# Attention weights transposed in pairs of tiles, eight transposes in a row, and multiplied with the values in pairs

## The chip, the cores and the metric

The kernel runs on one core of one Trainium2 chip. The metric is the device time of one execution in microseconds; the time of a kernel is the median over its runs. The engines are TensorE (PE in the profile, with PEld for its weight loads), VectorE (DVE), ScalarE (ACT), GpSimd (POOL) and SyncE (SP, which here only issues transfers).

## The reference

One layer with two kinds of heads over 2048 tokens of width 1024. The normalised input is projected once. Group A is stick-breaking attention with 16 heads of width 64, group B a chunked state-space scan; both are gated, normalised, and mapped back by one output projection. The change is in group A:

```python
z = jnp.einsum('bqhd,bkhd->bhqk', qi, kf) * scale
mask = key_pos[None, :] < q_pos[:, None]
log_keep = jnp.where(mask, jax.nn.log_sigmoid(-z), 0.0)
rest = lax.cumsum(log_keep, axis=3, reverse=True) - log_keep
w = jnp.where(mask, jnp.exp(jax.nn.log_sigmoid(z) + rest), 0.0)
return jnp.einsum('bhqk,bkhd->bqhd', w, vf)
```

A query reads the keys before it from the nearest to the farthest, and each key takes a sigmoid share of what the nearer ones left. The kernel computes this with a scan over the keys that runs backwards: the scanned value `w` is what has been given to all keys up to one place, and the values are taken as differences of neighbouring rows, so that `w` itself can be multiplied with them.

## The kernel before

The program has three stages: the state-space group of the first 1024 tokens with its projections, then `attention` (L450), then the state-space group of the other half and the output projection. Only `attention` is concerned.

**Segments.** Attention goes through 32 segments `(H, p, q)` (L452): the half `H` of the tokens, the pair of heads `p`, and the block `q` of 512 queries in that half. For each of the two heads of a pair it goes over the key tiles of 512 keys, from the block's own (the diagonal one) back to the first, `Q + 1` of them with `Q = 2 * H + q`. A key tile has four steps, one for each 128 queries. That makes 8, 16, 24 or 32 steps in a segment and 640 in all.

**A step**, `z_step` (L594), computes one tile of 128 queries by 512 keys: two products into a bank `z` of PSUM (L601, L602; on the diagonal a third one adds the mask, L604), two sigmoids on ACT (L606 into `be`, L607 in place in `z`), and the scan on DVE (L610), which reads both and writes `w`. `z` has two banks, so a score waits until the scan of two steps before is over. On the diagonal the tiles are narrower: 128, 256, 384 and 512 keys.

**Transposes**, `t_step` (L615). Before `w` meets the values, its keys must lie on the partitions. For each 128 keys `j` of a key tile, PE transposes the 128 columns of the four `w` of that tile, four transposes into one bank `t` (L619; fewer on the diagonal). ACT casts the bank to `th` in fp32r (L622), DVE subtracts to get the rest `tl` (L624), and then the bank is free. There are two banks `t`, and the projection stage uses the same two for its own transposes of queries and keys (L524, with L530 and L531 to empty them).

**Products with the values**, `av_step` (L632): `V` with `th` (L636) and with `tl` (L637), added up in the bank `av` over all key tiles of a head. There is one such bank. At the end of a head ACT copies one half of it into `y` (L642), DVE adds the other (L643), and only then may the next head's first product write.

**The order.** Each step puts its `j` into the queue `tq`. `advance` (L654), called once a step, takes the oldest entry for a transposition as soon as six wait (`LAG`), and then multiplies the oldest transposed tile as soon as more than two of them wait (`AVLAG`). So a step issues one score, one group of four transposes, and two products. Between the steps `fill` brings in work of the next segments, by a balance of estimated times (L701 to L705): the projection of queries, keys and values (L473 to L475, bank `pj`), the gate (L245 to L247), the transposes of `stage_b`. The last segments have little or none of it. The instructions then pass a scheduler, which orders each engine's instructions ahead of time; on the chip each engine keeps that order.

The numbers of banks and the two lags stand here:

```python
PSB = {"z": 2, "t": 2, "av": 1, "pj": 3}
LAG = 6
AVLAG = 2
```

Of the kernel before, what the change touches and what calls it, by code (L numbers as in the profile page):

```python
# [30 lines left out]
LAG = 6  # L31
# [4 lines left out]
UNIT = 0.55  # L36
CS = (0, 2, 4)
FF = (1.05, 1.35)
AVLAG = 2


def f32(t):
    return t.bitcast(F32)
# [3 lines left out]
def hybrid_layer_kernel(ctx: ExitStack, tc: tile.TileContext, x, norm_w, wA, wP0, wP, wZ, wdt, vec, w_out, out):  # L47
# [16 lines left out]
    def ps(tag):  # L64
        return psum.tile([P, 512], F32, name=tag, bufs=PSB[tag])
# [171 lines left out]
    def projector(hx):  # L237
        hh, hl = [h[0] for h in hx], [h[1] for h in hx]

        def proj_steps(pj, wts, cs, q, m=P):  # L240

            wh, wl = wts
            for kt in range(KT):
                a, b = wh[kt][:, cs], wl[kt][:, cs]
                te.matmul(pj[:m], a, hh[q][:, kt, :], start=(kt == 0), stop=False)  # L245
                te.matmul(pj[:m], a, hl[q][:, kt, :], start=False, stop=False)  # L246
                te.matmul(pj[:m], b, hh[q][:, kt, :], start=False, stop=(kt == KT - 1))  # L247
                yield

        def proj_t(wts, cs, q, m=P):  # L250
            pj = ps("pj")
            drain(proj_steps(pj, wts, cs, q, m))
            return pj
        return proj_t, proj_steps
# [195 lines left out]
    def attention(ap_, wp, hp, hx):  # L450
# [164 lines left out]
        def t_step(h, c, j, ws):  # L615
            lo = j if c == h.Q else 0
            tp = ps("t")
            for i in range(lo, 4):
                te.transpose(tp[:, i * P:(i + 1) * P], ws[i][:, j * P:(j + 1) * P], ident)  # L619
            rs = slice(lo * P, 512)  # L620
            th = ap_.tile([P, 512], F32R, name="th", bufs=4)
            sc.copy(th[:, rs], tp[:, rs])  # L622
            tl = ap_.tile([P, 512], F32R, name="tl", bufs=3)
            ve.tensor_tensor(tl[:, rs], tp[:, rs], f32(th[:, rs]), op=ALU.subtract)  # L624
            if lo == 3:

                gp.memset(f32(th[:, 256:384]), 0.0)
                gp.memset(f32(tl[:, 256:384]), 0.0)
                rs = slice(256, 512)
            return th, tl, rs  # L630

        def av_step(h, c, j, V, tt):  # L632
            th, tl, rs = tt
            if c == h.Q and j == 0:
                h.av = ps("av")
            te.matmul(h.av[:, rs], V[:, j, :], th[:, rs], start=(c == h.Q and j == 0), stop=False)  # L636
            te.matmul(h.av[:, rs], V[:, j, :], tl[:, rs], start=False, stop=(c == 0 and j == 3))  # L637
            if c == 0 and j == 3:
                own = slice(h.e * 64, h.e * 64 + 64)
                oth = slice(64 - h.e * 64, 128 - h.e * 64)  # L640
                y = h.y
                sc.copy(y[own], h.av[oth])  # L642
                ve.tensor_tensor(y[own], h.av[own], y[own], op=ALU.add)  # L643
                gp.tensor_mul(y[own], y[own], h.gz[own])  # L644
                if h.e == 1:
                    nc.sync.dma_start(ysb_d[h.p, :, h.Q * 512:(h.Q + 1) * 512], y)
# [5 lines left out]
        tq, aq = [], []  # L652

        def advance():  # L654
            if len(tq) >= LAG:
                h, c, j, ws, V = tq.pop(0)
                aq.append((h, c, j, V, t_step(h, c, j, ws)))
            if len(aq) > AVLAG:
                av_step(*aq.pop(0))

        for n, (H, p, q) in enumerate(segs):
            fill = fill_for(n)
# [24 lines left out]
            for e in range(2):  # L687
                h = Head()
                h.p, h.e, h.Q, h.y, h.gz = p, e, Q, y, gzs[H, p, q]
                h.AB = made[H, p, q][0][e]  # L690
                prev = [None] * 4
                for c in range(Q, -1, -1):
                    if todo:
                        fetch(*todo.pop(0))
                    M, V = mv.pop((e, c))
                    ws = []
                    for i in range(4):
                        z_step(h, c, i, M, ws, prev)
                        tq.append((h, c, i, ws, V))
                        advance()  # L700
                        due += scale * tau[step % len(tau)] - core[step % len(tau)]  # L701
                        step += 1
                        while due >= UNIT:
                            next(fill, None)
                            due -= UNIT  # L705
            drain(fill)
        while tq or aq:
            if aq:
                av_step(*aq.pop(0))
            if tq:  # L710
                h, c, j, ws, V = tq.pop(0)
# [73 lines left out]
    with tc.tile_pool(name="sp1", bufs=1, side="right") as sp:  # L785
        chunks, gates, _ = ssd(1, sp, wp, *projector(hx))
# [67 lines left out]
```

## Time and profile before

| | |
|---|---|
| Median of 3 runs | 2744.19 us (2741.96 to 2746.96) |
| The profiled execution | 2747.84 us, its span 2745.6 us |
| PE busy | 2592.6 us, 94% of the span |
| PE's weight loads busy | 2138.9 us, 78% |
| DVE busy | 2016.6 us, 73% |
| ACT busy | 1647.5 us, 60% |
| POOL busy | 845.8 us, 31% |
| Scans (L610, 128x512, with a carried value) | 384 of 1278 ns, 490.7 us |
| Transposes of attention weights (L619) | 2176, 346.6 us |
| Casts to `th` (L622) | 640, 339.0 us |
| Subtractions to `tl` (L624) | 640, 376.9 us |

A matmul's start is recorded and its end is modelled; several are in the pipe at once. So the distance from one start to the next tells what a matmul costs, and its duration does not: the 2176 transposes have a mean duration of 275 ns, yet follow each other at 0.11 us. An idle time in brackets at the end of a row names what ended it.

### The profile page before, as it was taken

The numbers are of one execution on the slowest core, as the hardware profiler recorded it, in microseconds if no ns is written. First come the engines' busy times: TensorE is split into PE (matmuls) and PEld (weight loads), VectorE is DVE, ScalarE is ACT, GpSimd is POOL, SyncE is SP. The second block draws the span as 40 slices with busy tenths as digits, with TensorE's granted clock in tenths as the row PEclk, the third lists the DMA queues.
The fourth block names the chain that finished last, engine by engine and source line by source line (L and its number), as shares of the span: only waits on it lengthen the run. The fifth ranks groups of instructions, "written<-read, shape, count | busy, mean of one in ns | idle before, by whom it ended". The sixth has DMA issues, their size and how long they took to land.

```text
span 2745.6 us, 40149 instructions
## 1 busy us (share of the span) xinstructions
PE 2592.6 (94%) x13858; PEld 2138.9 (78%) x13858; DVE 2016.6 (73%) x3160; ACT 1647.5 (60%) x3551; POOL 845.8 (31%) x844
## 2 busy tenths in 40 slices
PE   7998999999999999999999999999999896989999
PEld 5876788888888778787878787877776774778877
DVE  6566337767776777968696868688997667877766
ACT  4557446666666666868686867677886456331221
POOL 1456232322333222121212121212112456351553
PEclk9999999999999999999999999999999998999999
DMA  3225642222322422122212121222121136574553
GB/s 114 62 74 144 228 122 65 78 76 83 93 81 86 116 73 70 58 81 58 81 55 85 53 86 51 84 56 74 57 70 39 49 94 184 184 219 146 153 166 115
DMA packets 207627, 265.16 MB, mean 97 GB/s; under 512 B 18384, under 2 KB 127200, under 8 KB 207424
## 3 DMA queue, kind: packets, MB, share of 16 engines
q1 hardware_dynamic: 188992, 229.04, 28.1%
q10 hardware_dynamic: 18432, 33.56, 4.2%
q8 instruction: 109, 1.79, 0.3%
q14 instruction: 94, 0.77, 0.1%
HBM read 178.00 MB, written 59.38 MB: 86 GB/s over the span
## 4 chain that ended last, share of the span: by engine, by line
PE 53%; DVE 25%; issue 7%; ACT 7%; DMA 4%; POOL 3%; SPq 0%; ACTq 0%; DVEq 0%; POOLq 0%
DVE w L610 8%; PE t L619 5%; PE pj L475 4%; PE pj L474 4%; PE pj L473 4%; DVE tl L624 4%; PE pj L247 3%; PE pj L246 3%; PE pj L245 3%; PE av L636 3%; PE z L601 3%; PE av L637 2%; PE z L602 2%; PE pj L762 2%; PE pj L760 2%
## 5 line engine op out<-in xcount | busy, mean ns | idle before, releaser
L610 DVE TENSOR_TENSOR_SCAN w<-z,w,be 128x512 f32<-128x512 f32 x384 | 490.7, 1278 | 135.1 <-ACT z L607 132.5
L606 ACT ACTIVATE be<-z 128x512 f32<-128x512 f32 (+3 forms) x640 | 343.7, 537 | 328.9 <-PE z L604 166.0
L624 DVE TENSOR_TENSOR tl<-t,th 128x512 fp32r<-128x512 f32 (+3 forms) x640 | 376.9, 589 | 9.5 <-ACT th L622 7.6
L622 ACT CAST th<-t 128x512 fp32r<-128x512 f32 (+3 forms) x640 | 339.0, 530 | 31.8 <-PE t L619 29.5
L619 PE MATMUL t<-ident,w 128*128 128x128 f32 x2176 | 346.6, 275 | 9.8 <-DVE tl L624 3.8
L473 PE MATMUL pj<-wh,hh 128*128 128x384 f32 (+1 forms) x1024 | 349.9, 342 | 0.0
L475 PE MATMUL pj<-wh,hl 128*128 128x384 f32 (+1 forms) x1024 | 346.8, 339 | 0.0
L474 PE MATMUL pj<-wl,hh 128*128 128x384 f32 (+1 forms) x1024 | 346.7, 339 | 0.0
L607 ACT ACTIVATE z<-z 128x512 f32<-128x512 f32 (+3 forms) x640 | 341.1, 533 | 0.2
L610 DVE TENSOR_TENSOR_SCAN w<-z,be 128x128 f32<-128x128 f32 (+3 forms) x256 | 209.8, 819 | 170.3 <-ACT z L607 141.3
L619 PEld LDWEIGHTS t<-ident,w 128*128 128x128 f32 x2176 | 255.1, 141 | 71.7 <-DVE tl L624 16.7
L133 POOL TENSOR_TENSOR wl<-wraw,wh 128x384 fp32r<-128x384 f32 (+3 forms) x163 | 169.4, 1050 | 440.8 <-ACT wh L132 238.7
L644 POOL TENSOR_TENSOR y<-y,gz 64x512 f32<-64x512 f32 x64 | 82.9, 1296 | 531.1 <-DVE y L643 530.6
L473 PEld LDWEIGHTS pj<-wh,hh 128*128 128x128 f32 x1024 | 192.9, 188 | 12.5 <-ACT hh L173 0.2
L474 PEld LDWEIGHTS pj<-wl,hh 128*128 128x128 f32 x1024 | 193.0, 189 | 12.0
L475 PEld LDWEIGHTS pj<-wh,hl 128*128 128x128 f32 x1024 | 193.0, 188 | 0.7
L246 PE MATMUL pj<-hl,zh 128*128 128x512 f32 x432 | 175.3, 406 | 0.0
L245 PE MATMUL pj<-hh,zh 128*128 128x512 f32 x432 | 173.3, 401 | 0.0
L247 PE MATMUL pj<-hh,zl 128*128 128x512 f32 x432 | 172.2, 399 | 0.0
L636 PE MATMUL av<-th,V 128*128 128x512 f32 (+2 forms) x384 | 155.3, 405 | 12.1 <-DVE y L643 11.2
L601 PE MATMUL z<-M,AB 128*128 128x512 f32 (+2 forms) x384 | 141.4, 368 | 10.7 <-DVE w L610 8.5
L637 PE MATMUL av<-tl,V 128*128 128x512 f32 (+2 forms) x384 | 141.1, 368 | 0.0
(244 smaller groups left out, 6060.5 us busy)
## 6 DMA issues: line engine op xcount, KB each, us to landing
wraw<-in_wP_dram SPq DMA_DIRECT2D x112, 192.0 KB, 2.5
wk<-acs_scr SPq DMA_DIRECT2D x64, 256.0 KB, 3.4
AB<-AB SPq DMA_DIRECT2D x128, 128.0 KB, 2.4
Mc<-kc_scr ACTq DMA_DIRECT2D x64, 256.0 KB, 2.7
Vc<-vc_scr ACTq DMA_DIRECT2D x64, 256.0 KB, 2.6
wraw<-in_wZ_dram SPq DMA_DIRECT2D x54, 256.0 KB, 2.6
wraw<-in_wA_dram SPq DMA_DIRECT2D x44, 192.0 KB, 2.3
ea<-acs_scr SPq DMA_DIRECT2D x32, 256.0 KB, 4.4
```

The lines of the kernel that those rows point to most:

```text
L245: te.matmul(pj[:m], a, hh[q][:, kt, :], start=(kt == 0), stop=False)
L246: te.matmul(pj[:m], a, hl[q][:, kt, :], start=False, stop=False)
L247: te.matmul(pj[:m], b, hh[q][:, kt, :], start=False, stop=(kt == KT - 1))
L473: te.matmul(pj[:, :n], a, wh[kt][:, 0:n], start=(kt == 0), stop=False)
L474: te.matmul(pj[:, :n], a, wl[kt][:, 0:n], start=False, stop=False)
L475: te.matmul(pj[:, :n], b, wh[kt][:, 0:n], start=False, stop=(kt == KT - 1))
L606: sc.activation(be[:, :nk], zp[:, :nk], AF.Sigmoid, scale=0.125)
L607: sc.activation(zp[:, :nk], zp[:, :nk], AF.Sigmoid, scale=-0.125)
L610: ve.tensor_tensor_scan(w[:, 0:nk][:, ::-1], zp[:, 0:nk][:, ::-1], be[:, 0:nk][:, ::-1], 0.0 if diag else prev[i][:, 0:1], ALU.mult, ALU.add)
L619: te.transpose(tp[:, i * P:(i + 1) * P], ws[i][:, j * P:(j + 1) * P], ident)
L622: sc.copy(th[:, rs], tp[:, rs])
L624: ve.tensor_tensor(tl[:, rs], tp[:, rs], f32(th[:, rs]), op=ALU.subtract)
```

## The change

`advance` waits until `tq` holds at least six entries and an even number. Then it first multiplies all tiles that are transposed (two of them), and then transposes two more. `AVLAG` goes. The queue so drains two steps' worth at every second step.

```diff
--- before.py
+++ after.py
@@ -36,7 +36,6 @@
 UNIT = 0.55
 CS = (0, 2, 4)
 FF = (1.05, 1.35)
-AVLAG = 2
 
 
 def f32(t):
@@ -652,11 +651,13 @@
         tq, aq = [], []
 
         def advance():
-            if len(tq) >= LAG:
-                h, c, j, ws, V = tq.pop(0)
-                aq.append((h, c, j, V, t_step(h, c, j, ws)))
-            if len(aq) > AVLAG:
-                av_step(*aq.pop(0))
+
+            if len(tq) >= LAG and len(tq) % 2 == 0:
+                while aq:
+                    av_step(*aq.pop(0))
+                for _ in range(2):
+                    h, c, j, ws, V = tq.pop(0)
+                    aq.append((h, c, j, V, t_step(h, c, j, ws)))
 
         for n, (H, p, q) in enumerate(segs):
             fill = fill_for(n)
```

From the deleted line up to `advance`, lines have a number less by one in the changed kernel: scores L600 and L601, scan L609, transposes L618, cast L621, subtraction L623, products L635 and L636.

Uninterrupted groups of attention transposes in the order of PE: 639 before (447 of four, one of seven, the others smaller, on the diagonal) and 451 after (103 of eight, 91 of seven, 32 of five or six, 48 of four, 177 smaller).

PE, a step of the last segment, where no other work is left. `Mc` and `V` are keys and values, `AB` the queries. Before:

```order
L601 MATMUL z<-Mc,AB 128x512
L602 MATMUL z<-Mc,AB 128x512
L619 MATMUL t<-ident,w 128x128 x4
L637 MATMUL av<-tl,V 128x512
L636 MATMUL av<-th,V 128x512
L601 MATMUL z<-Mc,AB 128x512
```

After, two steps:

```order
L600 MATMUL z<-Mc,AB 128x512
L601 MATMUL z<-Mc,AB 128x512
L635 MATMUL av<-th,V 128x512
L600 MATMUL z<-Mc,AB 128x512
L601 MATMUL z<-Mc,AB 128x512
L636 MATMUL av<-tl,V 128x512
L635 MATMUL av<-th,V 128x512
L618 MATMUL t<-ident,w 128x128 x2
L636 MATMUL av<-tl,V 128x512
L618 MATMUL t<-ident,w 128x128 x6
```

Each score was followed by a group of four and two products. Now two scores stand with one product between them, and all eight transposes behind the second score, with the rest of the products ahead of and among them.

DVE at the same place, with buffer numbers (the scan is shown as SCALAR_TENSOR_TENSOR). Before:

```order
L610 SCALAR_TENSOR_TENSOR w_23303<-z_23297,w_23222,be_23300 128x512
L624 TENSOR_TENSOR tl_23312<-t_23305,th_23310 128x512
L610 SCALAR_TENSOR_TENSOR w_23322<-z_23316,w_23244,be_23319 128x512
L624 TENSOR_TENSOR tl_23331<-t_23324,th_23329 128x512
L610 SCALAR_TENSOR_TENSOR w_23341<-z_23335,w_23266,be_23338 128x512
L624 TENSOR_TENSOR tl_23350<-t_23343,th_23348 128x512
```

After:

```order
L609 SCALAR_TENSOR_TENSOR w_23314<-z_23308,w_23236,be_23311 128x512
L609 SCALAR_TENSOR_TENSOR w_23322<-z_23316,w_23244,be_23319 128x512
L623 TENSOR_TENSOR tl_23335<-t_23328,th_23333 128x512
L623 TENSOR_TENSOR tl_23344<-t_23337,th_23342 128x512
L609 SCALAR_TENSOR_TENSOR w_23352<-z_23346,w_23276,be_23349 128x512
L609 SCALAR_TENSOR_TENSOR w_23360<-z_23354,w_23284,be_23357 128x512
```

Scan and subtraction took turns; now two scans are followed by two subtractions.

DVE at the end of a head, in a segment of two key tiles (650 to 694 us in the profile). The next head's first product stands on PE, in both kernels, behind the score that the scan of 128x512 reads; `y` is what it waits for. Before:

```order
L610 SCALAR_TENSOR_TENSOR w_6680<-z_6673,be_6677 128x384
L624 TENSOR_TENSOR tl_6688<-t_6682,th_6686 128x384
L643 TENSOR_TENSOR y_6199<-av_6573,y_6199 64x512
L610 SCALAR_TENSOR_TENSOR w_6711<-z_6704,be_6708 128x512
L624 TENSOR_TENSOR tl_6718<-t_6713,th_6716 128x256
```

After (`qkt` and `qky` are small steps of a normalisation, `raw` its last one):

```order
L609 SCALAR_TENSOR_TENSOR w_6651<-z_6644,be_6648 128x256
L105 SCALAR_TENSOR_TENSOR qkt_6611<-qkx_6609,qky_6610 128x16
L642 TENSOR_TENSOR y_6209<-av_6566,y_6209 64x512
L106 TENSOR_TENSOR qkt_6611<-qkt_6611,qky_6610 128x16
L623 TENSOR_TENSOR tl_6667<-t_6660,th_6665 128x512
L107 SCALAR_TENSOR_TENSOR qky_6610<-qkt_6611,qky_6610 128x16
L623 TENSOR_TENSOR tl_6675<-t_6669,th_6673 128x384
L501 TENSOR_TENSOR raw_6327<-raw_6327,qky_6610 128x1024
L609 SCALAR_TENSOR_TENSOR w_6693<-z_6686,be_6690 128x384
L609 SCALAR_TENSOR_TENSOR w_6711<-z_6704,be_6708 128x512
```

The addition to `y` stood between the scans of 128x384 and 128x512; now it stands one scan earlier, ahead of that of 128x384.

## Rows read from the trace of the kernel before

**Rows 1.** Windows, attention: us, busy time by engine, clock, DMA share, GB/s.
```profile
386.00:2101.00 1715.00, 1650.06 (x9276) 1392.81 (x9275) 1347.88 (x2033) 1215.48 (x2696) 390.11 (x455) 0.99 0.26 74
```

**Rows 2.** Windows: a segment of two key tiles, one of four.
```profile
650.00:694.00 44.00, 42.41 (x249) 37.10 (x248) 33.28 (x56) 30.73 (x73) 9.37 (x12) 1.00 0.18 50
...
1515.90:1584.30 68.40, 65.95 (x367) 53.52 (x367) 61.64 (x88) 56.00 (x121) 12.86 (x16) 1.00 0.19 55
```

**Rows 3.** Waits in attention, PE's weight loads: total us, times, longest.
```profile
PEld z L601 <- DVE w L610: 90.3, 170, 2.4
...
PEld av L636 <- DVE y L643: 23.3, 44, 0.9
PEld t L619 <- DVE tl L624: 16.7, 46, 1.4
...
PEld t L524 <- DVE tl L624: 3.9, 14, 0.8
```

**Rows 4.** Waits in attention: idle time of PE's products.
```profile
PE z L601 <- DVE w L610: 28.0, 76, 2.0
PE av L636 <- DVE y L643: 11.2, 24, 0.7
```

**Rows 5.** Timeline of PE (start, us, instruction): a group of four.
```profile
453.88 0.60 PE L619 MATMUL t<-ident,w 128*128 128x128 f32 x4
454.23 0.48 PE L636 MATMUL av<-th,V 128*128 128x512 f32 x1
454.55 0.39 PE L637 MATMUL av<-tl,V 128*128 128x512 f32 x1
454.78 0.33 PE L473 MATMUL pj<-wh,hh 128*128 128x384 f32 x1
```

**Rows 6.** Timeline of PE: a run of eight.
```profile
479.93 1.04 PE L524 MATMUL t<-ident,raw 128*128 128x128 f32 x8
480.73 0.36 PE L601 MATMUL z<-M,AB 128*128 128x256 f32 x1
480.93 0.28 PE L602 MATMUL z<-M,AB 128*128 128x256 f32 x1
481.05 0.23 PE L604 MATMUL z<-maskb,identb 128*128 128x128 bf16 x1
```

**Rows 7.** Timeline: from a head's last product to the next head's first.
```profile
655.30 0.28 PE L637 MATMUL av<-tl,V 128*128 128x256 f32 x1
...
656.35 0.59 ACT L642 COPY y<-av 64x512 f32<-64x512 f32 x1
...
657.44 0.53 DVE L624 TENSOR_TENSOR tl<-t,th 128x384 fp32r<-128x384 f32 x1
...
657.89 0.67 DVE L643 TENSOR_TENSOR y<-av,y 64x512 f32<-64x512 f32 x1
...
658.62 0.50 PE L636 MATMUL av<-th,V 128*128 128x512 f32 x1 [0.69 <-DVE y L643]
```

**Rows 8.** Waits of weight loads, segment 1515.9 to 1584.3 us.
```profile
PEld av L636 <- DVE y L643: 1.0, 2, 0.8
```

**Rows 9.** Timeline, all engines: a step where DVE paces.
```profile
2059.24 0.50 PE L601 MATMUL z<-Mc,AB 128*128 128x512 f32 x1
2059.24 0.59 ACT L622 CAST th<-t 128x512 fp32r<-128x512 f32 x1
...
2059.68 1.27 DVE L610 TENSOR_TENSOR_SCAN w<-z,w,be 128x512 f32<-128x512 f32 x1
...
2060.01 0.60 ACT L606 ACTIVATE be<-z 128x512 f32<-128x512 f32 x1 [0.17 <-PE z L602]
...
2060.50 0.59 ACT L607 ACTIVATE z<-z 128x512 f32<-128x512 f32 x1
...
2060.87 0.66 DVE L624 TENSOR_TENSOR tl<-t,th 128x512 fp32r<-128x512 f32 x1
...
2061.45 1.27 DVE L610 TENSOR_TENSOR_SCAN w<-z,w,be 128x512 f32<-128x512 f32 x1
```

## The prediction

> **What bounds the kernel now.** I read the busy time by stretch first. Attention is 1715.0 us of the 2745.6 us span, and PE is busy for 1650.06 us of it at a granted clock of 0.99 of full speed, the 2.4 GHz level, so transposes between the products do not lower the clock today [rows 1]. The rest of the program is not touched. Inside attention two kinds of segments differ (a segment is one pair of heads and 512 queries). In a first-half segment of two key tiles, 650 to 694 us, PE is busy for 42.41 of 44.00 us and DVE for 33.28: PE paces it. In a second-half segment of four key tiles, 1515.9 to 1584.3 us, DVE is busy for 61.64 of 68.40 us, and over long pieces it has no gap: DVE paces those [rows 2].
>
> Then I read who makes PE wait, in the waits of its weight loads over attention, since each product begins with one. Scores wait for a scan to release their `z` bank: 90.3 us in 170 waits. The first product with the values of a new head waits for `y` of the head before, because the `av` bank is single: 23.3 us in 44 waits. Transposes wait for a subtraction that releases their `t` bank: 16.7 us in 46 waits, and those of the projection stage 3.9 us in 14 [rows 3]. A weight load starts while the product ahead still streams, so these are upper bounds. The idle time of PE itself, 28.0 us and 11.2 us for the first two, is the lower bound [rows 4].
>
> **The change, part by part.** The multiplications, casts, subtractions, scans and transfers are the same in number and size. What moves is their order: pairs of tiles instead of single ones.
>
> *Fewer switches between transposes and products.* Of 639 uninterrupted groups of attention transposes 451 remain, so 188 switches go. What is one worth? A group of four at 453.88 us ends in a dear first product: `av` takes 0.32 us from its start to the next (454.23 to 454.55), the one behind it 0.23 us (454.55 to 454.78), so 0.09 us seems to be lost at the switch. But the first product also starts early, 0.35 us after the first of four transposes. The whole group costs 454.55 - 453.88 - 0.23 = 0.44 us, or 0.11 us a transpose [rows 5]. The kernel already has runs of eight without a wait. One starts at 479.93 us; the score behind it starts at 480.73 and the next at 480.93, and a score of this width takes 0.12 us (480.93 to 481.05): 480.93 - 479.93 - 0.12 = 0.88 us, again 0.11 us each [rows 6]. Two groups of four cost 0.88 us, one of eight 0.88 us. The 0.09 us is part of the last transpose and not a toll of the switch. By the rows' rounding of 0.02 us the term is 188 x 0.02 = 4 us at most either way; I take **0**.
>
> *The wait for `y`.* Today the last product of a head and the first of the next stand one step apart. At 655.30 us the last product runs; `y` is copied on ACT at 656.35, added on DVE at 657.89 behind a subtraction, and the next head's first product starts only at 658.62, 3.32 us later [rows 7]. In the new order the last two tiles of a head close one pair, and the next head's first product comes in the next pair, two steps later. A step of that segment lasts 44.00 / 16 = 2.75 us, so the pair leaves about 5.5 us for a chain of 3.3 us: the wait should go. Of its 23.3 us, the eight DVE-paced segments (second half, four key tiles) hold 1.0 us each [rows 8], 8 us that DVE would take back. What is left is 15 us: **-15** (bounds 0 and -23).
>
> *The waits for `t` banks.* Single groups collide today with the projection stage's own transposes, which hold the same two banks. Pairs come half as often but want both banks. Together the two waits are 16.7 + 3.9 = 20.6 us [rows 3]; I take half of it: **-10** (bounds 0 and -21; the other sign is the first rival).
>
> *The scores' waits.* Where DVE paces, a step is one scan and one subtraction: 2059.68 to 2061.45 us, 1.77 us, with no gap [rows 9]. In the new order DVE does scan, scan, subtraction, subtraction: 3.54 us a pair, the same work. The 90.3 us are mostly PE waiting for an engine that is full, and they stay: **0** (at best the 28.0 us of idle PE, nothing taken).
>
> Does the new order keep DVE full? Behind the second subtraction of a pair, which frees the second `t` bank, PE has one product left (0.32 us) and six transposes (0.66 us), then the next score. From a score's start to its `be` on ACT is 0.77 us (2059.24 to 2060.01), to the second sigmoid 0.49 us more, and that one lasts 0.59 us [rows 9]: 0.32 + 0.66 + 1.85 = 2.83 us, 2.9 with hand-overs. DVE has 3.54 us of work in that time. The slack is 0.6 us. In stretches with projection work PE paces a pair at 5.5 us, and there is more.
>
> The Trainium skill ("Perfetto Trace Analysis", Optimizing Tensor Performance, on matmuls) says that independent groups should rotate through PSUM banks, so that the emptying of one overlaps the filling of the next. That speaks against this change, which fills both `t` banks in one go; by it the sum would be the first rival's and not mine.
>
> Sum: 0 - 15 - 10 + 0 = **-25 us**. The profiled execution took 2747.84 us, so 2722.8 us; it stands 3.65 us above the median of the runs shown (2744.19), so I predict **2719 us** for a median. With every term at its better bound short of the scores' it would be -48 us, 2696.
>
> **The rivals.**
>
> *A. DVE runs dry behind the pair.* The mechanism is the loop above: second subtraction, last product, transposes, score, two sigmoids, scan. If it grows by more than the slack of 0.6 us, each pair opens a gap on the engine that paces. ACT could do that: it now has two casts of `th` in a row (0.59 us each) behind four sigmoids, and weight casts squeeze in. The 170 waits of scores mark about 85 pairs in DVE-paced stretches; 0.5 us beyond the slack in each is 43 us: 2719 + 43 = 2762, slower. For it: the slack is small, and the order is fixed ahead of time, so it cannot adapt. Against it: the first cast needs only the first four transposes, and the cast ends before the score's sigmoid could start. Chance 0.16.
>
> *B. The switch is a toll after all.* If the 0.09 us behind each group goes with 188 groups, that is 17 us more: 2702. The run of eight speaks against it. Chance 0.07.
>
> *C. The waits only change their name.* `y` and the banks no longer hold PE, but DVE or ACT end the same steps as late, as in the segments where DVE is at 61.64 of 68.40 us. Then about 5 us remain: 2739, no change. For it: 256 of the 640 steps are in segments of four key tiles, where DVE is dense. Against it: in the first half PE is the only dense engine. Chance 0.15.
>
> *D. The clock falls.* At present the granted clock is 0.99 in attention, and eight transposes in a row at 479.93 us keep their pace. If the clock sank to the 1.2 GHz level for the transposes in each of the 226 groups of five and more, each would lose as much again as its 0.87 us: 197 us, 2916. Chance 0.02. The Trainium skill ("TensorE: Matmul & The Clock Gate", Part 4 on PE-mode transposes) says that transposes do not count as activity for the full clock, which would point this way; the run of eight in rows 6 does not show it.
>
> **How the numbers follow.** My forecast has 0.60, B 0.07, C 0.15, A 0.16, D 0.02. A measurement of this kernel tells 0.2% from no change, 5.5 us: faster means under 2738.7, slower over 2749.7. The forecast and B are faster, 0.67; C is the same, 0.15; A and D are slower, 0.18. The range goes from 2696, all better bounds without the scores', to 2752, which takes in C and the mild part of A; what lies outside is the rest of A, D, and a gain in the scores' waits, under 0.2 together.
>
> **What would show it.** In the profile of the changed kernel the waits of PE's weight loads for `y` should be under 8 us in place of 23.3, and those of `t` for a subtraction about half. A group of eight should still cost 0.88 us, and products behind it 0.32 us. The segments of two key tiles should shrink from 44 us by about 2 us; those of four from 68.4 us by less than 1.5 us. DVE in the last segment should still run without gaps, now scan, scan, subtraction, subtraction in 3.54 us. I am wrong if scans wait there for the second sigmoid (A), if a run of eight costs 0.80 us or less (B), if the segments of two key tiles stay at 44 us (C), or if the granted clock over attention drops below 0.97 (D).

## The result, and the profile after

The changed kernel takes 2783.41 us in the median where the kernel before takes 2746.96 in the same job: ratio 1.0135, 95% interval 1.012 to 1.015, **slower by 37 us**. One of the changed kernel's five runs took 4134.71 us at a granted clock of 0.655; the ratio is of the other four. The prediction (2719 us, faster) has the wrong sign, and the time lies outside its range. The profiled execution took 2779.29 us.

All of it is lost in attention: 1751.1 us from the start of its first score to that of its last product, against 1715.1. Windows of the changed kernel, first attention, then a segment of two key tiles and one of four, answering to [rows 1, 2] (same columns; the engines stand in the order PE, PEld, DVE, ACT, POOL):

```profile
386.00:2137.00 1751.00, 1656.56 (x9273) 1405.97 (x9273) 1392.40 (x2034) 1209.56 (x2694) 380.74 (x455) 0.99 0.25 72
648.10:691.10 43.00, 41.93 (x248) 37.18 (x246) 33.47 (x54) 30.49 (x70) 9.16 (x12) 1.00 0.15 43
1533.10:1604.50 71.40, 67.51 (x374) 54.90 (x372) 63.18 (x88) 56.85 (x123) 15.19 (x18) 1.00 0.22 60
```

The clock is the same. A segment of two key tiles became 1 us shorter, one of four 3 us longer. And DVE is busy for 44.5 us more with the same work (1392.40 against 1347.88), which no term of the prediction had.

Waits of PE's weight loads in attention of the changed kernel, answering to [rows 3] ("issue" is time for which the profile names no releaser):

```profile
PEld z L600 <- DVE w L609: 100.2, 153, 3.2
...
PEld t L618 <- issue: 26.3, 16, 2.5
PEld av L636 <- DVE tl L623: 15.5, 35, 2.2
PEld t L523 <- DVE tl L623: 14.9, 17, 4.5
PEld t L618 <- DVE tl L623: 5.1, 8, 0.8
```

Idle time of PE's products there, answering to [rows 4]:

```profile
PE z L600 <- DVE w L609: 46.8, 110, 2.9
PE t L618 <- DVE AB L530: 19.7, 13, 2.1
PE t L523 <- DVE tl L623: 9.3, 9, 4.1
PE av L636 <- DVE tl L623: 7.9, 22, 1.9
```

The rows of the kernel before that answer to the waits for `t` banks, one of its weight loads and two of its products:

```profile
PEld t L619 <- issue: 8.2, 13, 0.7
PE t L619 <- DVE AB L531: 2.8, 12, 0.3
PE t L524 <- DVE tl L624: 0.8, 2, 0.5
```

The wait for `y` is gone from both lists. In its place PE stands idle for `t` banks: 19.7 us in only 13 waits where it was 2.8 in 12, and 9.3 us where it was 0.8. All such waits together were 13 us and are 34. Scores stand 46.8 us for scans in place of 28.0, and products with the values now stand 7.9 us for a subtraction, which they did not before.

A group of eight transposes in the changed kernel (timeline of PE), answering to [rows 5, 6], and the steady pair in the last segment (timeline of DVE), answering to [rows 9]:

```profile
673.07 1.03 PE L618 MATMUL t<-ident,w 128*128 128x128 f32 x8
673.86 0.42 PE L472 MATMUL pj<-wh,hh 128*128 128x384 f32 x1
674.12 0.34 PE L473 MATMUL pj<-wl,hh 128*128 128x384 f32 x1
```

```profile
2093.83 1.26 DVE L623 TENSOR_TENSOR tl<-t,th 128x512 fp32r<-128x512 f32 x2
...
2095.01 2.45 DVE L609 TENSOR_TENSOR_SCAN w<-z,w,be 128x512 f32<-128x512 f32 x2
...
2097.38 1.26 DVE L623 TENSOR_TENSOR tl<-t,th 128x512 fp32r<-128x512 f32 x2
```

The eight cost 674.12 - 673.07 - 0.17 = 0.88 us, as predicted (0.17 us is what a later product of this width takes, 653.32 to 653.49 us in the rows of runs 11 and 12). The pair on DVE takes 2097.38 - 2093.83 = 3.55 us without a gap: rival A's mechanism is not there, in this segment.

Where a `t` wait comes from shows at 1480 us. Timeline, all engines, of the changed kernel:

```profile
1480.10 1.03 PE L523 MATMUL t<-ident,raw 128*128 128x128 f32 x8
...
1482.14 0.67 ACT L529 ACTIVATE AB<-t,vt 64x512 fp32r<-64x512 f32 x1
...
1486.33 0.76 DVE L530 SCALAR_TENSOR_TENSOR AB<-t,vt,AB 64x512 fp32r<-64x512 f32 x1
...
1487.23 0.41 PE L618 MATMUL t<-ident,w 128*128 128x128 f32 x2 [2.07 <-DVE AB L530]
```

And PE, with one row of DVE, at the like place of the kernel before:

```profile
1464.53 0.60 PE L524 MATMUL t<-ident,raw 128*128 128x128 f32 x4
1466.34 0.63 PE L524 MATMUL t<-ident,raw 128*128 128x128 f32 x4
...
1469.81 0.76 DVE L531 SCALAR_TENSOR_TENSOR AB<-t,vt,AB 64x512 fp32r<-64x512 f32 x1
...
1470.71 0.41 PE L619 MATMUL t<-ident,w 128*128 128x128 f32 x2 [0.28 <-DVE AB L531]
```

In the changed kernel the projection stage fills both `t` banks in one run of eight. They are emptied by ACT and DVE between sigmoids and scans, and the last part of the first bank is out only 7 us later; the next attention weights have waited 2.07 us for it. Before, the first bank was held for 6.0 us as well (1464.53 to 1470.57 us). But the two groups of four came apart, with products between them, and the next transposes waited 0.28 us: the bank was free 1 us sooner, and PE reached them 0.8 us later. This one pause recurs: six segments of three key tiles have it with 1.93 to 2.07 us, seven of two key tiles with 1.06 or 1.07. Together they are the 19.7 us.

Most of DVE's 44.5 us lies in the small steps of the normalisation of queries and keys (128x16, nine of them Newton steps, which refine a reciprocal square root). Groups of DVE by line, before and then after (busy us, mean ns):

```profile
L106 DVE SCALAR_TENSOR_TENSOR qkt<-qkx,qky 128x16 f32<-128x16 f32 x93 | 24.1, 259 | 2.1
L107 DVE TENSOR_TENSOR qkt<-qkt,qky 128x16 f32<-128x16 f32 x93 | 24.1, 259 | 1.4
L108 DVE SCALAR_TENSOR_TENSOR qky<-qkt,qky 128x16 f32<-128x16 f32 x93 | 26.3, 283 | 1.9
```

```profile
L105 DVE SCALAR_TENSOR_TENSOR qkt<-qkx,qky 128x16 f32<-128x16 f32 x93 | 42.4, 456 | 2.1
L106 DVE TENSOR_TENSOR qkt<-qkt,qky 128x16 f32<-128x16 f32 x93 | 31.0, 333 | 1.9
L107 DVE SCALAR_TENSOR_TENSOR qky<-qkt,qky 128x16 f32<-128x16 f32 x93 | 43.6, 469 | 1.9
```

The same 279 instructions went from 74.5 to 117.0 us; counting all eleven small steps of a normalisation, from 96.4 to 128.5, 32 us more. Timeline of DVE, POOL and PE, changed kernel, where it costs most:

```profile
1031.08 0.17 DVE L107 SCALAR_TENSOR_TENSOR qky<-qkt,qky 128x16 f32<-128x16 f32 x1
1031.11 1.31 POOL L544 TENSOR_TENSOR V<-vd,V 128x512 fp32r<-128x512 f32 x1
1031.29 1.17 DVE L105 SCALAR_TENSOR_TENSOR qkt<-qkx,qky 128x16 f32<-128x16 f32 x1
...
1036.02 0.68 DVE L609 TENSOR_TENSOR_SCAN w<-z,be 128x256 f32<-128x256 f32 x1
...
1036.75 0.50 PE L600 MATMUL z<-M,AB 128*128 128x512 f32 x1 [2.90 <-DVE w L609]
```

A small step takes 0.17 us, but where POOL works on a tensor, it ends with POOL's instruction (1031.29 + 1.17 against 1031.11 + 1.31 us). The scan stands behind them on DVE, and PE waits 2.90 us for it. By the overlap of the records (over 0.04 us, fills by POOL not counted), 82 of the 341 small steps had POOL work beside them before (mean 0.64 us) and 115 after (0.79 us); the others have a mean of 0.17 us in both.

### The profile page after: what moved, and what is told of

The parts are those of the page before. It is cut to its first block, busy times and chain, and to the rows that moved or that the text cites. A ratio compares the mean times of both kernels' runs of the same rounds, so it can differ in the third digit from the quotient of the medians.

```text
span 2777.6 us, 40287 instructions
## 1 busy us (share of the span) xinstructions
PE 2598.2 (94%) x13858; PEld 2151.2 (77%) x13858; DVE 2060.3 (74%) x3160; ACT 1642.2 (59%) x3551; POOL 838.1 (30%) x844
## 4 chain that ended last, share of the span: by engine, by line
PE 47%; DVE 24%; issue 12%; ACT 8%; DMA 5%; POOL 3%; SPq 0%; DVEq 0%; POOLq 0%; ACTq 0%
DVE w L609 8%; PE pj L472 4%; PE pj L474 4%; PE pj L473 4%; PE t L618 4%; PE pj L246 3%; PE pj L245 3%; PE pj L244 3%; DVE tl L623 3%; PE z L600 2%; PE av L636 2%; PE av L635 2%; PE z L601 2%; PE pj L763 2%; ACT z L606 2%
## 5 line engine op out<-in xcount | busy, mean ns | idle before, releaser
L609 DVE TENSOR_TENSOR_SCAN w<-z,w,be 128x512 f32<-128x512 f32 x384 | 485.6, 1276 | 125.9 <-ACT z L606 123.2
L623 DVE TENSOR_TENSOR tl<-t,th 128x512 fp32r<-128x512 f32 (+3 forms) x640 | 361.4, 599 | 41.3 <-ACT th L621 40.0
L621 ACT CAST th<-t 128x512 fp32r<-128x512 f32 (+3 forms) x640 | 309.3, 529 | 116.0 <-PE t L618 111.6
L472 PE MATMUL pj<-wh,hh 128*128 128x384 f32 (+1 forms) x1024 | 366.7, 358 | 0.0
L618 PE MATMUL t<-ident,w 128*128 128x128 f32 x2176 | 312.7, 273 | 22.8 <-DVE AB L530 19.7
L618 PEld LDWEIGHTS t<-ident,w 128*128 128x128 f32 x2176 | 259.1, 140 | 67.0 <-issue 26.3
L609 DVE TENSOR_TENSOR_SCAN w<-z,be 128x128 f32<-128x128 f32 (+3 forms) x256 | 207.3, 818 | 127.6 <-ACT z L606 125.6
L244 PE MATMUL pj<-hh,zh 128*128 128x512 f32 x432 | 180.2, 417 | 0.0
L600 PE MATMUL z<-M,AB 128*128 128x512 f32 (+2 forms) x384 | 145.1, 378 | 17.1 <-DVE w L609 16.3
L636 PE MATMUL av<-tl,V 128*128 128x512 f32 (+2 forms) x384 | 137.3, 363 | 7.9 <-DVE tl L623 7.9
L600 PE MATMUL z<-Mc,AB 128*128 128x512 f32 x256 | 113.9, 445 | 31.5 <-DVE w L609 30.5
```

The costliest lines, as they stand in the source:

```text
L472: te.matmul(pj[:, :n], a, wh[kt][:, 0:n], start=(kt == 0), stop=False)
L600: te.matmul(zp[:, :nm], h.AB[:, 0, isl], M[:, :nm], start=True, stop=False)
L609: ve.tensor_tensor_scan(w[:, 0:nk][:, ::-1], zp[:, 0:nk][:, ::-1], be[:, 0:nk][:, ::-1], 0.0 if diag else prev[i][:, 0:1], ALU.mult, ALU.add)
```

## The experiments

**Theories.** T: the `t` banks, which pairs of groups take two at a time. V: the pairs of products. N: the normalisation's small steps, in one block beside POOL's work. R: what is left is the order of scores and products itself. S: the mask's product in bf16, which now stands ahead of other products. "pj" below is the same edit in both kernels; it gives the projection stage's transposes other banks. What is measured is given as the ratio to the kernel before, with its 95% interval; 0.001 is 2.7 us.

**Runs 1 and 2: one half of the change each.** Transposes in pairs alone, then products in pairs alone (for the body of `advance`):

```diff
+            if len(tq) >= LAG and len(tq) % 2 == 0:
+                for _ in range(2):
+                    h, c, j, ws, V = tq.pop(0)
+                    aq.append((h, c, j, V, t_step(h, c, j, ws)))
+            if len(aq) > 2:
+                av_step(*aq.pop(0))
```


> One part alone: transposes in pairs as in the change, products with the values one tile a step as before. Theory T (a pair of groups wants both t banks at once and so collides with the projection stage's own transposes, about 20 us of the 36 us lost): the loss is there with the pairs of transposes alone, ratio to before 1.008 or more, and the waits of weight loads for t banks stay over 40 us. Theory V (the products in pairs are the harm, because four products stand together and their tiles come late): this kernel is at 1.000 to 1.004. The wait for y: the last tiles of a head are multiplied one a step, so part of the 23 us returns, under 15 us in both theories.

```diff
+            if len(tq) >= LAG:
+                if len(aq) == 3:
+                    av_step(*aq.pop(0))
+                    av_step(*aq.pop(0))
+                h, c, j, ws, V = tq.pop(0)
+                aq.append((h, c, j, V, t_step(h, c, j, ws)))
```


> The other part alone: groups of four transposes one a step as before, products with the values two tiles at every second step. Theory T: the t banks are used as before, their waits stay at 15 to 25 us, and the ratio to before is 1.000 +- 0.004. Theory V: ratio 1.008 or more. The next head's first product stands two steps behind the last product, as in the change, so the wait for y should be under 8 us in both.

Measured 1.0033 (1.0023 to 1.0042) and 1.0029 (1.0017 to 1.0040). Neither theory is met (the first ratio is under T's range, the second under V's): each half alone loses 8 to 9 us, both together 37. The wait for `y` stayed with the first (27.8 us, more than expected) and went with the second (3.5 us): the pairs of products cure it. Waits for `t` banks rose in both.

**Runs 3 and 4: other banks for the projection stage, after and before.**

```diff
             for qk in range(2):
-                tp = ps("t")
+                tp = ps("pj")
```


> The changed kernel, but the projection stage's transposes of queries and keys go through the pj banks, so that t banks serve the attention weights alone. Theory T: most of the loss through t banks goes, 15 to 25 us faster than the changed kernel, ratio to before 1.000 to 1.007. Theory N (the small normalisation steps stand in one block in DVE's order, meet POOL's work and get slower, and scans wait behind them): t banks matter little, under 8 us, ratio still over 1.010. The pj banks are then asked for by one more user, so some waits for pj can come instead, in both theories.

> The control: the kernel before with the same move of the projection stage's transposes to the pj banks. Before, these collisions were small (3.9 us in 14 waits of the projection stage's transposes), so theory T expects 0.997 to 1.003 against before; theory N the same. A gain or loss here is the price of the move itself and is taken off the run above.

Measured 1.0026 (1.0015 to 1.0037) for the changed kernel and 1.0006 (0.9995 to 1.0017) for the kernel before. The gap between the two orders falls from 0.0135 to 0.0020: sharing the `t` banks costs the change 0.0115, 32 us. PE's idle time in attention of run 3 says the same:

```profile
PE z L600 <- DVE w L609: 52.6, 116, 2.9
...
PE pj L523 <- DVE gz L511: 4.1, 6, 1.1
...
PE t L618 <- DVE hl L173: 0.6, 2, 0.4
```

The waits for `t` banks are nearly gone; 4.1 us of waits for a `pj` bank have come. The scores' waits are not gone, and the nine small steps still take 117.7 us (72.1 in run 4).

**Runs 5 and 6: no Newton steps, after and before, both with pj.**

```diff
-        for _ in range(3):
+        for _ in range(0 if tag == "qk" else 3):
```


> The changed kernel with the projection stage's transposes in the pj banks, and without the nine small Newton steps (128x16) of each normalisation of queries and keys; this leaves out the refinement of the reciprocal square root. Those steps took 118 us of VectorE in the run with pj banks against 72 us in the same move of the kernel before. Theory N (the block of small steps, lengthened beside POOL, holds up the scans, and that is the 7 us that remain): this run and its partner without the steps from the kernel before come within 3 us of each other. Theory R (what remains comes from the order of scores and products itself): the gap stays at 5 to 9 us. Against before: 30 to 60 us faster, ratio 0.980 to 0.992.

> The partner: the kernel before with the pj move and without the same Newton steps (the refinement of the reciprocal square root is left out). Theory N: gains less than its partner, since its steps were shorter and spread among other work, ratio 0.985 to 0.995. Theory R: gains the same as its partner, so that 5 to 9 us lie between them.

Measured 0.9898 (0.9882 to 0.9915) and 0.9912 (0.9897 to 0.9927). The gap of 0.0020 turns to -0.0014: the steps cost the change's order 0.0034 more, 9 us, with an uncertainty of about 8 us (the half-widths of the four ratios are 0.0011 to 0.0017). That speaks for theory N and against R, without settling the size. The traces say where: in the segments of the second half (three and four key tiles, sums in the table further down) run 3 stands 18.5 us behind run 4, run 5 only 2.1 us behind run 6. PE's idle time of scores for scans is another matter. Without the steps it is still 38.6 us in run 5 against 22.0 in run 6 (52.6 against 29.9 with them), most of it in the segments of four key tiles, and yet run 5 is not the slower one.

**Runs 7 and 8: the Newton steps on POOL.** The kernel before, and the changed one with pj:

```diff
+        if tag == "qk":
+            gp.tensor_scalar(xv, xv, -0.5, 0.0, ALU.mult, ALU.add)
+            for _ in range(3):
+                gp.tensor_tensor(t, xv, y, op=ALU.mult)
+                gp.tensor_tensor(t, t, y, op=ALU.mult)
+                gp.tensor_scalar(t, t, 1.5, 0.0, ALU.add, ALU.add)
+                gp.tensor_tensor(y, t, y, op=ALU.mult)
+            return y
```


> A candidate: the kernel before with the Newton steps of the queries' and keys' normalisation on POOL (one more step each, since POOL multiplies and adds in separate instructions), where only 390 of 1715 us are busy. If these steps cost time because DVE carries them, 72 us of DVE work leave and the kernel gains 10 to 30 us, ratio 0.989 to 0.997. If POOL's steps hold DVE up as its larger ones do, or the longer chain makes the next queries late, nothing is gained, ratio 0.998 to 1.005.

> The same for the changed kernel with the pj banks. Theory N: gains more than the kernel before does by this, and ends within 3 us of it. Theory R: keeps its 5 to 9 us behind it. If POOL's small steps lengthen DVE's work as its large ones seem to, subtractions and scans grow by 10 us or more in sum.

Measured 1.0264 (1.0248 to 1.0279) and 1.0150 (1.0134 to 1.0165), both far slower than expected. Run 8 ends 31 us ahead of run 7, which meets neither N (within 3 us) nor R (5 to 9 us behind); run 7 also lacks the pj move. DVE by line in run 7:

```profile
L510 DVE TENSOR_TENSOR raw<-raw,qky 128x1024 f32<-128x1024 f32 x31 | 59.7, 1924 | 106.3 <-POOL qky L111 106.3
```

DVE's multiplication by the result waits 106.3 us for POOL, and whatever stands behind it on DVE waits as well. POOL's steps take 0.20 to 0.27 us each; that they queue behind its own long instructions is likely and was not tried. DVE had been relieved, and stood still.

**Run 9, and 14 to 16: the small steps handed out among the attention steps.** Run 9 yields between them as if each were projection work (`units` 42 to 52); the others pop two from a queue in each step (the lines that fill the queue are left out):

```diff
                         advance()
+                        for _ in range(2):
+                            if nq:
+                                nq.pop(0)()
```


> The changed kernel with the pj move, and with the nine Newton steps of each normalisation handed out one by one between the attention steps in place of all at once (all work is done). Theory N: fewer of the small steps meet a POOL operation and scans no longer stand behind the whole block; from 1.0026 it falls by 5 to 12 us, ratio 0.998 to 1.001. If the block as such does no harm, only the steps' total time beside POOL, the ratio stays at 1.001 to 1.005.

> The changed kernel with the pj move; the Newton steps are handed out two an attention step, as in the spread version, but without counting as projection work, so that the balance of scores and projections stays as it was. Theory N: 1.0026 falls to 0.998 to 1.001. If the spread version was slower because of the steps' places and not because of the changed balance, this one is slower than 1.0026 too.

> The partner: the kernel before with the pj move and the same handing out. Its steps were spread already in part, so it gains less, 0.997 to 1.001.

> Products in pairs, the pj move and the handing out together. If the three gains add, ratio 0.992 to 0.997; if the scores' waits take them back, 0.998 to 1.003.

Measured 1.0078 (1.0066 to 1.0090), 1.0070 (1.0057 to 1.0082), 1.0059 (1.0047 to 1.0071) and 1.0010 (1.0002 to 1.0019). None helps: the same kernels without it stand at 1.0026 (runs 9 and 14), 1.0006 (run 15) and 0.9984 (run 16). In run 9 the three Newton lines fell to 70.8 us, but the false projection units moved real projection work: segments of one key tile took 258 us in sum in place of 280, those of two 390 in place of 353. It decides nothing about N. In run 14 the lines take 121 us, as in run 3 (118): handing the steps out in the program did not part them from POOL's work. That the block does harm by its place, apart from the time that it takes, stays open.

**Run 10: the wait for `y` by a longer lag.** The kernel before with pj:

```diff
-AVLAG = 2
+AVLAG = 3
```


> The wait for y by itself: the kernel before with the pj move, groups and products one a step, but products one step later (AVLAG 3 in place of 2). If the wait for y is worth what the prediction took (15 us), the next head's first product still stands one step behind the last one, so the wait stays (20 us in 30 or more waits) and the time is that of the pj move alone, ratio 0.998 to 1.003; only the waits for th (10.2 us in 13) should go. If it is the lag and not the pairs that cures y, the wait falls under 10 us and the ratio is 0.994 to 0.998.

Measured 1.0049 (1.0038 to 1.0061), slower than both expectations. The waits for `y` became fewer, not shorter in sum (17 of up to 2.4 us, 23.3 in all): lag is no cure.

**Runs 11 and 12: no mask product, after and before, both with pj.**

```diff
-            te.matmul(zp[:, :nm], h.AB[:, 1, isl], M[:, :nm], start=False, stop=not diag)
-            if diag:
-                te.matmul(zp[:, isl], identb, maskb, start=False, stop=True)
+            te.matmul(zp[:, :nm], h.AB[:, 1, isl], M[:, :nm], start=False, stop=True)
```


> The changed kernel with the pj move, without the product that adds the mask on the diagonal (the mask is left out: 256 products of 128 columns in bf16). Theory S (in the order of the change a projection or score product stands behind the mask product, and is 0.085 us dearer there; behind a transpose it was not): this kernel gains 256 x 0.04 us and some 7 us more than its partner from the kernel before. Without theory S both gain the same 8 to 15 us.

> The partner: the kernel before with the pj move and without the mask's product (the mask is left out). It gains 8 to 15 us against the pj move alone (1.0006), ratio 0.995 to 0.998. The difference between this and the run above, against that between the two runs with the mask (0.0020, 5.5 us), is the price of the switch.

Measured 0.9942 (0.9930 to 0.9954) and 0.9946 (0.9933 to 0.9959): the gap falls from 0.0020 to -0.0004, 7 us with an uncertainty about as large. The partner's gain, 16 us, is a little more than was expected; the changed kernel gained 23. What the mask's neighbours cost is read from the timeline of PE, before and then after:

```profile
654.78 0.23 PE L604 MATMUL z<-maskb,identb 128*128 128x128 bf16 x1
654.85 0.50 PE L619 MATMUL t<-ident,w 128*128 128x128 f32 x3
```

```profile
653.01 0.23 PE L603 MATMUL z<-maskb,identb 128*128 128x128 bf16 x1
653.05 0.42 PE L472 MATMUL pj<-wh,hh 128*128 128x384 f32 x1
653.32 0.34 PE L473 MATMUL pj<-wl,hh 128*128 128x384 f32 x1
653.49 0.34 PE L474 MATMUL pj<-wh,hl 128*128 128x384 f32 x1
```

The product behind the mask takes 0.27 us from its start to the next where the following one takes 0.17. Before, 206 of the 256 mask products stood ahead of a transpose, after 4. A step of this kind costs 0.04 + 0.27 - 0.17 - 0.07 = 0.07 us more; 202 of them would be 14 us where PE never waits, and the runs show about half. The sign of S is likely, its size is not settled.

**Runs 13, 17 and 18: what is worth keeping.** Products in pairs as in run 2, with pj; then only in segments of two and three key tiles; then only in those of two (`Q == 1`):

```diff
-        def advance():
+        def advance(Q, step):
+            pair = Q in (1, 2)
+            while pair and step % 2 == 0 and len(aq) > 1:
+                av_step(*aq.pop(0))
             if len(tq) >= LAG:
...
-            if len(aq) > AVLAG:
+            while not pair and len(aq) > AVLAG:
                 av_step(*aq.pop(0))
```


> The products in pairs alone (as in the second run: transposes one group a step) with the projection stage's transposes in the pj banks. Products in pairs took the wait for y from 23.3 to 3.5 us and left 35 us of waits for t banks; the pj move should take most of those. If waits that end on PE are worth their length, this beats the kernel before by 5 to 12 us, ratio 0.995 to 0.998. If what the waits give back turns into waits of scores for scans (they were 96.2 us in the second run, 90.3 before), the ratio is 0.999 to 1.003.

> From the kernel before with the pj move: products with the values two tiles at every second step only in the segments of two and of three key tiles, where TensorE paces, and one a step elsewhere; transposes one group a step everywhere. By the segments of the runs so far (products in pairs against the pj move alone): two key tiles 343 against 361 us in sum, three 534 against 536, one 282 against 276, four 550 against 539. If these add segment by segment, the time is that of the pj move less 20 us: ratio 0.992 to 0.995. If what a segment gains is only moved work that its neighbour gets, the ratio is 0.997 to 1.001.

> The same, with products in pairs in the segments of two key tiles alone. If segments add: the pj move less 18 us, ratio 0.993 to 0.996. If a gain only moves work: 0.997 to 1.001.

Measured 0.9984 (0.9973 to 0.9995), 0.9961 (0.9949 to 0.9974) and 0.9962 (0.9948 to 0.9975). The last two beat the kernel before by 10 to 11 us. The sums over the eight segments of each kind, taken in the traces from the start of a segment's first score to that of the next segment's (us; the first half of the tokens has one and two key tiles, the second three and four). Each row is a single execution; that of run 4 is 5 us faster than its median, that of run 18 3 us slower:

| key tiles | one | two | three | four |
|---|---|---|---|---|
| before | 274.8 | 363.9 | 534.2 | 542.2 |
| after | 283.2 | 357.5 | 546.3 | 564.1 |
| after, pj (run 3) | 279.6 | 352.9 | 539.5 | 553.9 |
| before, pj (run 4) | 275.5 | 361.3 | 536.0 | 538.9 |
| after, pj, no Newton steps (5) | 270.2 | 348.3 | 518.6 | 549.2 |
| before, pj, no Newton steps (6) | 267.7 | 354.9 | 526.7 | 539.0 |
| products in pairs, pj (13) | 281.7 | 343.4 | 534.1 | 550.1 |
| the same, two key tiles only (18) | 283.6 | 342.0 | 539.2 | 540.0 |

In run 18 the segments of two key tiles gain 19 us against run 4, and those of one and three give 11 of them back: segments do not add, as the expectation of 18 to 20 us had taken it; 12 us is what the ratios show. The change itself loses 2.0 us in the first half of the tokens and 34.0 in the second.

## Why the prediction was wrong

By the gaps of the runs the 37 us are made up so: `t` banks +32 (runs 3, 4), Newton steps +9 (runs 5, 6), the mask's neighbours +7 (runs 11, 12), and the rest, about -10, which would hold the cured wait for `y`. Each is uncertain by 6 to 8 us. The `t` banks are shown with their control; that the three add up was not tried, the Newton steps and the mask are barely clear of the uncertainty, and the rest is a difference that no run measured.

*Fewer switches: right.* Eight transposes cost 0.88 us. But only the switch between transposes and products was looked at; the mask's switch, which had been hidden ahead of the transposes, was left out of the sum.

*The wait for `y`: right in mechanism, high in size.* It is gone, and products in pairs are its cure (3.5 us in run 2). With the banks apart they are worth 6 us in all segments (0.9984 against 1.0006) and 12 us where only the segments of two key tiles have them (0.9962), each uncertain by about 5 us; 15 were taken. That all of this comes from `y` was not tried by itself.

*The waits for `t` banks: the step that failed.* "Pairs come half as often but want both banks. I take half of it: -10 (bounds 0 and -21)." A loss was not within the bounds; the other sign was left to rival A, which is another mechanism. Its 20.6 us counted only waits for a subtraction; the row of `t` banks that grew most, transposes that wait for the projection stage to empty a bank (2.8 us of idle PE in 12 waits), was not in it. And waits of before are no bound for a new order: collisions that were short while groups of four came apart (0.28 us) became pauses of 1 to 2 us when one stage filled both banks in one run of eight. PE's idle time there went up by 21 us (13 to 34); the runs price the sharing at 32 us, and the other 11 us are not seen as idle time at the banks. The rule that the prediction quoted from the Trainium skill ("Perfetto Trace Analysis", Optimizing Tensor Performance) spoke for this loss; the 2.07 us at 1487.23 us agree with it, though through another user of the banks and not through the pair itself.

*The scores' waits: 0 taken.* They rose (idle 28.0 to 46.8 us). In one place scans stand behind the small steps (2.90 us at 1036.75), but most of the gap between the two orders stays when the steps are left out (runs 5, 6), and there it costs no time that the ratios show. DVE's lengthened small steps had no term at all.

*Where DVE paces.* The prediction took the segments of four key tiles to be paced by DVE alone and expected them to gain less than 1.5 us each. Its own [rows 2] have PE busy for 65.95 of 68.40 us, longer than DVE, and these segments lost most, 21.9 us in sum.

*Rivals.* A gave the right side (2762), but not by its mechanism. The pair keeps its 3.55 us in the last segment. Summed over the segments of four key tiles, scans wait 42.1 us for the second sigmoid where it was 31.6, but with the banks apart 33.1 (run 3) against 32.9 (run 4): the loop by itself does not open a gap. B and D are not seen: 0.88 us for eight, clock 0.99. C is seen in part. The segments of two key tiles did shrink, to 43 us (42 was predicted), but products in pairs alone, with the banks apart, gain 18 us there and lose 11 in the segments of four (run 13 against run 4).

## What to carry to other kernels

When work is bunched, list every user of the buffers that the bunch takes at once, and price the collision from how long the slowest of them holds a buffer (here 7 us), not from the waits of the old order. Then undo the bunching one half at a time: the half that cures the wait (products in pairs, where PE paces) was worth 12 us once the other half was left out and the banks were not shared; used in every segment it was worth 6.

## What was not expected of the hardware

A DVE instruction on 128x16 takes 0.17 us. In the changed kernel 81 of the 341 small steps took 0.54 to 2.05 us, and every one of these ended within 0.06 us of a POOL instruction on 128x384 to 128x512 that ran beside it. The Trainium skill ("SBUF — State Buffer", SBUF: two separate sides) says that DVE and POOL share one pair of ports, held by one of them for a whole instruction, and that a DVE instruction with two inputs in SBUF needs it when the POOL instruction reads SBUF; the step that ends with POOL's at 1032.4 us agrees, and so do the scans, which read one input from PSUM and keep 1.27 us, the 99 of 128x512 beside POOL's work too. No run took POOL's work away, so the cause itself was not tried. A product in fp32r behind the bf16 product of the mask costs about 0.1 us more from its start to the next (0.27 against 0.17 us at 653 us); the first one behind transposes is dearer by 0.09 us in the same way [rows 5], but starts early.
